# Two products of four column pairs at the head of the up projection, and the first query loads ahead of two stores

## The chip, the cores and the metric

The kernel runs on one core of a Trainium2 chip. The metric is device time in microseconds of one launch. Before the change it is 1542.04 us, the median of three runs (1541.46 to 1542.32). Engines are named as in the profile: PE is TensorE's matmul stream, PEld its weight loads, DVE is VectorE, ACT is ScalarE, POOL is GpSimd, and SP issues nearly all DMAs.

## The reference, cut to what matters

One encoder layer on 1024 prompt frames and 32 sample frames, that is 1056 frames of 1024 features, all in float32:

```
h = rmsnorm(x, g_mix); proj = h @ w_in          # queries, keys, values, conv parts, branch gates
y_attn = stick_breaking(q, k, v) @ w_attn_out;  y_conv = (cb * conv(cc * cx)) @ w_conv_out
x = x + (sigmoid(ga) * y_attn + sigmoid(gc) * y_conv) @ w_o
x = x + square(relu(rmsnorm(x, g_ffn) @ w_up)) @ w_down      # w_up: 1024 x 4096
x = x + sigmoid(rmsnorm(x, g_ple) @ w_ple_gate) * (p @ w_ple)
y = rmsnorm(x, g_final)
```

The change touches the product with w_up and, in its small part, the start of attention.

## The kernel before, in words

**Numbers.** A float32 product is made of three TensorE passes. Each operand is split into a high part (a rounded copy, on ScalarE) and a low part (what is left, a subtraction on VectorE); the passes are high by high, high by low and low by high. So each weight block costs a cast (L107, or L164 for half of one) and a subtraction (L108, L166). In the names `whi` and `wlo`, `sh` and `sl` are these parts.

**Tiles.** Features lie on the 128 partitions, frames in the free dimension. The 1056 frames are two halves of 528, a half is two quarters of 264 (`halves`, `quarters`; t = 0, 1 counts the quarters that belong together).

**The scheme of seven products.** w_up is 1024 x 4096. Two neighbouring blocks of 128 columns are a *set* (or pair); there are 16 sets, u0 to u15. In a set weights and activations are 2 x 2 blocks: A11 and A12 are the even and odd feature blocks of the first column block, A21 and A22 those of the second; B11 and B12 are the even features of the first and the second half of frames, B21 and B22 the odd features. The plain way takes eight block products. The function `seven` (L221) takes seven (Strassen–Winograd) with sums of weights S1 to S4, made on GpSimd by `prepare` (L181, its L203), and sums of activations T1 to T4. A product is 12 matmuls of 128 x 264 (four feature blocks by three passes), and each is done for t = 0 and 1. The order is A11·B11, S1·T1, S2·T2, A12·B21, S3·T3, S4·B22, A22·T4. The product A11·B11 is copied to SBUF as `p1`, and is needed again because S2·T2, S3·T3 and A22·T4 are accumulated in the PSUM bank that holds it (`ps_A11u`). S1·T1 (copied as `s5`) keeps another bank for S4·B22. `u2` is the copy of the first bank after S2·T2. VectorE combines these into the four result blocks C11, C12, C21, C22, in tiles `m1` (first column block) and `m2`; ScalarE takes relu and square, the last block's relu straight from PSUM (`last` is `relu2`, L1467).

**Behind a set.** The down projection is done in the same scheme, so each set also forms its activation sums: `mid_sums` (L1473) does four operations on VectorE, three of them between the two quarters of A22·T4. Blocks and sums are stored to DRAM tiles that `md` names, and read again by the down projection.

**The head of the up projection.** Set 0 is done the plain way (`up_plain`, L1487) with eight block products, 192 matmuls into `ps_up` banks, because the T sums aren't ready when the output projection (w_o, L1385 to L1387, `ps_wo`) ends. Sets 1 to 15 are done with seven. `operands` (L1322) makes the four kinds of B blocks from the residual rows `xr`, one pair of them for each of the eight feature blocks, the last behind the end of the output projection; `square` of the same rows (`sq`) feeds the means for the norm. `mean_squares` (L1443) takes three sums on TensorE, three TENSOR_SCALAR and eight RECIPROCAL on VectorE, starting 14 steps after set 1 has begun.

**What sets the order.** All of it is written out by hand (`manual_schedule`): each engine runs its instructions in the order in which the code emits them. `run` takes a body step by step (a step is a product of one t), and after each step advances each generator in the list `side`: the weight preparation of the next set, whose splits stand at steps given by tables (AT1 for set 1), fetches, T sums, means. A DMA queue of SP is in order as well, so a store that waits for its data holds the loads behind it.

**The start of attention.** The last gate rows of the input projection are stored to DRAM (`gd`, L1129). Then `keys_values` loads the first keys and values, and in the next stage `queries` (L777 to L779) loads the first queries for the scores `z` (L791).

## Time and profile before

| | |
|---|---|
| runs, median | 1542.04 us |
| the profiled execution | 1541.38 us, span 1539.7 us |
| granted TensorE clock, mean | 0.998 |
| busy: PE, DVE, ACT, POOL | 99%, 69%, 49%, 21% of the span |
| DMA | 173 GB/s over the span |

The span runs from the first to the last instruction; the profiled execution's own time is 1.7 us more. The up projection begins 766.4 us into the span. A row of a group of instructions gives line, engine, operation, output and input tile by the program's names with numbers left out (`u0` becomes `u`), partitions x elements, type, and the count. In a row of the timeline the first number is the start in us, the second the duration; in brackets stands the idle time of the engine ahead of it and what ended that. A row of waits gives the idle time, its count and the mean. Line numbers are those of the kernel before, unless it says "of the changed kernel".

### The profile page before, as it was taken

The numbers are of one execution on the slowest core, as the hardware profiler recorded it, in microseconds if no ns is written. First come the engines' busy times: TensorE is split into PE (matmuls) and PEld (weight loads), VectorE is DVE, ScalarE is ACT, GpSimd is POOL, SyncE is SP. The second block draws the span as 40 slices with busy tenths as digits, with TensorE's granted clock in tenths as the row PEclk, the third lists the DMA queues.
The fourth block names the chain that finished last, engine by engine and source line by source line (L and its number), as shares of the span: only waits on it lengthen the run. The fifth ranks groups of instructions, "written<-read, shape, count | busy, mean of one in ns | idle before, by whom it ended". The sixth has DMA issues, their size and how long they took to land.

```text
span 1539.7 us, 29459 instructions
## 1 busy us (share of the span) xinstructions
PE 1518.7 (99%) x11816; PEld 1506.5 (98%) x11816; DVE 1067.1 (69%) x1441; ACT 750.5 (49%) x1371; POOL 317.6 (21%) x340
## 2 busy tenths in 40 slices
PE   8999999999999999999999999999999999999997
PEld 7999999999999999999999999999999999999997
DVE  7568656657578887775577555545577986789756
ACT  6544444434456664432355555555543334434644
POOL 2223322231112221002312222221020220000253
PEclk9999999999999999999999999999999999999999
DMA  6513445413748633445354444344886897683433
GB/s 226 202 48 118 187 153 193 166 44 130 236 125 257 207 123 124 147 167 182 128 191 140 146 147 152 131 143 155 303 281 205 279 332 241 198 275 120 141 127 117
DMA packets 110568, 268.94 MB, mean 175 GB/s; under 512 B 12992, under 2 KB 30144, under 8 KB 110432
## 3 DMA queue, kind: packets, MB, share of 16 engines
q1 hardware_dynamic: 110144, 266.75, 51.3%
q8 instruction: 92, 1.51, 0.4%
q14 instruction: 44, 0.36, 0.1%
q10 hardware_dynamic: 288, 0.32, 0.1%
HBM read 186.31 MB, written 80.72 MB: 173 GB/s over the span
## 4 chain that ended last, share of the span: by engine, by line
PE 63%; DVE 0%; ACT 0%; issue 0%; DVEq 0%
PE ps_dn L1696 7%; PE ps_dn L1698 7%; PE ps_dn L1697 7%; PE ps_A11u L217 4%; PE ps_A11u L216 4%; PE ps_A11u L218 4%; PE ps_pg L116 2%; PE ps_wo L1387 2%; PE ps_wo L1386 2%; PE ps_wo L1385 2%; PE ps_pg L118 2%; PE ps_pg L117 2%; PE ps_S1u L217 2%; PE ps_S1u L218 2%; PE ps_S1u L216 2%; PE ps_oa L116 1%
## 5 line engine op out<-in xcount | busy, mean ns | idle before, releaser
L1698 PE MATMUL ps_dn<-fh,wlo_dn 128*128 128x264 f32 x896 | 255.0, 285 | 0.0
L1696 PE MATMUL ps_dn<-fh,whi_dn 128*128 128x264 f32 x896 | 254.8, 284 | 0.0
L1697 PE MATMUL ps_dn<-fl,whi_dn 128*128 128x264 f32 x896 | 254.5, 284 | 0.0
L1696 PEld LDWEIGHTS ps_dn<-fh,whi_dn 128*128 128x128 f32 x896 | 168.8, 188 | 0.0
L1698 PEld LDWEIGHTS ps_dn<-fh,wlo_dn 128*128 128x128 f32 x896 | 168.6, 188 | 0.0
L1697 PEld LDWEIGHTS ps_dn<-fl,whi_dn 128*128 128x128 f32 x896 | 168.6, 188 | 0.0
L203 POOL TENSOR_TENSOR s_i<-raw_i,raw_i 128x512 f32<-128x512 f32 x32 | 43.6, 1363 | 239.9 <-DVE slS_i L166 209.8
L809 DVE TENSOR_TENSOR_SCAN r<-r 128x128 f32<-128x128 f32 (+3 forms) x64 | 86.4, 1351 | 4.1 <-POOL r L802 4.1
L1583 ACT CAST whi_dn<-raw_dn 128x1024 fp32r<-128x1024 f32 x40 | 42.0, 1051 | 83.5 <-PE ps_dn L1697 83.5
L203 POOL TENSOR_TENSOR s_u<-raw_u,raw_u 128x512 f32<-128x512 f32 x30 | 44.1, 1470 | 182.7 <-DVE slS_u L166 171.0
L1589 DVE TENSOR_TENSOR wlo_dn<-raw_dn,whi_dn 128x1024 fp32r<-128x1024 f32 x40 | 61.3, 1532 | 28.4 <-ACT whi_dn L1583 28.4
L216 PE MATMUL ps_A11i<-T,shS_i 128*128 128x264 f32 x256 | 73.1, 285 | 0.0
L218 PE MATMUL ps_A11i<-T,slS_i 128*128 128x264 f32 x256 | 72.9, 285 | 0.0
L217 PE MATMUL ps_A11i<-T,shS_i 128*128 128x264 f32 x256 | 72.7, 284 | 0.0
L849 DVE TENSOR_TENSOR at<-pa,at 128x512 fp32r<-128x512 f32 (+2 forms) x96 | 52.0, 551 | 26.7 <-ACT at L848 22.2
L1609 DVE TENSOR_TENSOR fl<-mr,fh 128x1056 fp32r<-128x1056 f32 x56 | 70.0, 1249 | 0.3 <-ACT q L1649 0.3
L166 DVE TENSOR_TENSOR slS_i<-s_i,shS_i 128x512 fp32r<-128x512 f32 x48 | 35.1, 737 | 49.7 <-ACT shS_i L164 49.5
L802 POOL TENSOR_SCALAR_AFFINE_SELECT r<-r 128x128 f32<-128x128 f32 x64 | 30.4, 475 | 187.8 <-ACT r L795 176.4
L1780 POOL TENSOR_TENSOR xx<-xx,pgs 128x384 f32<-128x384 f32 (+1 forms) x23 | 24.2, 1057 | 216.8 <-DVE pgs L1779 210.1
L216 PE MATMUL ps_A11u<-T,shS_u 128*128 128x264 f32 x240 | 68.4, 285 | 0.0
L217 PE MATMUL ps_A11u<-T,shS_u 128*128 128x264 f32 x240 | 68.4, 285 | 0.0
L218 PE MATMUL ps_A11u<-T,slS_u 128*128 128x264 f32 x240 | 68.1, 284 | 0.0
(451 smaller groups left out, 5582.9 us busy)
## 6 DMA issues: line engine op xcount, KB each, us to landing
raw_dn<-in_w_down_dram SPq DMA_DIRECT2D x56, 512.0 KB, 4.5
raw_i<-in_w_in_dram SPq DMA_DIRECT2D x36, 512.0 KB, 4.6
mr<-mdT SPq DMA_DIRECT2D x32, 528.0 KB, 5.5
raw_u<-in_w_up_dram SPq DMA_DIRECT2D x32, 512.0 KB, 3.5
mdB<-m SPq DMA_DIRECT2D x48, 264.0 KB, 2.5
mr<-mdB SPq DMA_DIRECT2D x24, 528.0 KB, 6.2
raw_pg<-in_w_ple_gate_dram SPq DMA_DIRECT2D x17, 512.0 KB, 3.6
mdT<-ta SPq DMA_DIRECT2D x32, 264.0 KB, 2.1
```

Of the source, the lines that this page charges most:

```text
L116: nc.tensor.matmul(ps, wh, xh[k][:, cols], start=(k == order[0]), stop=False)
L203: f()
L216: nc.tensor.matmul(p_, wh[:, k, :], o[:, 0, c], start=new and n == 0, stop=False, **on)
L217: nc.tensor.matmul(p_, wh[:, k, :], o[:, 1, c], start=False, stop=False, **on)
L218: nc.tensor.matmul(p_, wl[:, k, :], o[:, 0, c], start=False, stop=z, **on)
L809: nc.vector.tensor_tensor_scan(rev, rev, rev, 1.0, ALU.mult, ALU.bypass)
L849: nc.vector.tensor_tensor(al, pt[:, :nb, :], ah.bitcast(F32), op=ALU.subtract)
L1589: dve(lo, raw, hi.bitcast(F32), op=sub)
L1609: dve(l, mraw.pop(v), opd[v].bitcast(F32), op=sub)
L1696: nc.tensor.matmul(ps, hi[:, j, :], oh, start=j == 0, stop=False)
L1697: nc.tensor.matmul(ps, hi[:, j, :], ol, start=False, stop=False)
L1698: nc.tensor.matmul(ps, lo[:, j, :], oh, start=False, stop=j == NP_ - 1)
```

## The change

**Head of the up projection.** `up_plain` goes; `up_early` takes its place. It does two products of each of the first four sets, which need only B11 and B21: P = A11·B11 and C = A12·B21 on top of it in the same bank, in the order P0, P1, C0, C1, P2, C2, P3, C3. P is copied by ScalarE into a tile that is kept (`pe`, `held_p`). After C the bank holds C11; relu and square are taken, and the block goes to DRAM and is loaded again into `m1` when its set comes. The raw weights are split whole (`early_split`): the first set's in the last block of the output projection, the others' after P0, C1 and P2 of t = 0. The operands B12 are not made any more, and the last feature block's order of B21 and B22 is no longer turned round.

**Sets 0 to 3** then run in `seven`'s new branch with the five other products, 120 matmuls, S1·T1 first; S2·T2 starts a bank of its own. Since the kept P isn't in the bank, it is added or subtracted in SBUF on VectorE: in `s5` and `u2`, and in C21, which VectorE now writes as bank + P (L304 of the changed kernel) before ScalarE takes the relu from SBUF. The weight sums of set 0 are prepared during `up_early`, those of sets 1 to 3 at the steps of a new table AT2. Sets 4 to 15 are as before.

**First queries.** The two stores of the last gate rows are emitted behind the first two calls of `queries`.

```diff
-AT1 = (5, 4, 6, 7, 8, 12)
+AT1 = (5, 4, 6, 8, 10, 12)
+NEARLY = 4
+AT2 = (4, 6, 8, 10, 12, 15)
...
+    def early_split(s_):
+        early_w[s_] = even_odd(load_w(None, 0, KD, f"e{s_}", raw=early_raw.pop(s_)))
+    def early_first(s_, t):
+        p_ = early_ps[s_, t] = products(f"e{s_}_{t}", ((early_w[s_][0], "B11"),), quarters[t])
+        nc.scalar.copy(held_p[s_][:, quarters[t]], p_)
+    def early_second(s_, t):
+        p_ = early_ps.pop((s_, t))
+        products("", ((early_w[s_][1], "B21"),), quarters[t], p_)
+        return p_
...
+        if s_ in held_p:
+            p1 = [held_p[s_][:, quarters[t]] for t in range(2)]
+            for t, a, b in q:
+                z[t] = product("S1", "T1", t)
+                nc.scalar.copy(s5[t], z[t])
+                yield
+            for t, a, b in q:
+                x[t] = product("S2", "T2", t)
+                nc.scalar.copy(u2[t], x[t])
+                dve(s5[t], s5[t], p1[t], op=sub)
+                yield
         for t, a, b in q:
             product("S3", "T3", t, x[t])
+            if s_ in held_p:
+                dve(u2[t], u2[t], p1[t], op=add)
             dve(m2[:, b], x[t], s5[t], op=sub)
...
             product("A22", "T4", t, x[t])
-            last(m2, a, x[t])
+            if s_ in held_p:
+                dve(m2[:, a], x[t], p1[t], op=add)
+                last(m2, a)
+            else:
+                last(m2, a, x[t])
...
         queries(0, 0, 0)
         queries(0, 0, 1)
+        for i, m in enumerate(last_m[1]):
+            nc.sync.dma_start(gd[last_m[0] + i], m)
...
-        by_half = list(zip(halves, ("B21", "B22") if n % 2 else ("B11", "B12")))
-        for c, k in by_half[::-1] if n == KD - 1 else by_half:
+        for c, k in zip(halves, ("B21", "B22") if n % 2 else ("B11",)):
...
-                prepare_plain("u0", 0)
+                early_split("u0")
...
+    def up_early():
+        order = [("P", 0), ("P", 1), ("C", 0), ("C", 1), ("P", 2), ("C", 2), ("P", 3), ("C", 3)]
+        splits = {("P", 0): 1, ("C", 1): 2, ("P", 2): 3}
+        for k, i in order:
...
+            for t in range(2):
+                if k == "P":
+                    early_first(s_, t)
+                else:
+                    p_ = early_second(s_, t)
+                    relu2(c11[i], quarters[t], p_)
+                if t == 0 and (k, i) in splits:
+                    early_split(f"u{splits[k, i]}")
+                yield
+            if k == "C":
+                nc.scalar.square(c11[i], c11[i])
+                nc.sync.dma_start(md("B11", i), c11.pop(i))
...
-        side += [prepare("u1", AT1), all_t(), after(3, call(fetch_up, 2))]
-        run(up_plain())
+        side += [all_t(), after(1, call(fetch_up, 0)), after(3, prepare("u0", AT1)), after(7, call(fetch_up, 1))]
+        run(up_early())
         x1.clear()
         side.append(after(14, mean_squares()))
-        for s_ in range(1, NSET):
+        for s_ in range(NSET):
             if s_ + 1 < NSET:
-                side.append(prepare(f"u{s_ + 1}"))
+                side.append(prepare(f"u{s_ + 1}", AT2) if s_ + 1 < NEARLY else prepare(f"u{s_ + 1}"))
```

Three places in the engines' queues follow; line numbers are those of the kernel that the rows are from. First ScalarE around the end of the output projection. `xr7` is the last residual row, `B22_3` and `B21_3` its operands, `sq7` its square. Before:

```order
L1398 ACTIVATE sq6_9364<-xr6_9015 128x1056
L107 CAST whi_u0_1_9482<-raw_u0_1_9219 128x1024
L1329 ACTIVATE B22_3_9421<-xr7_9121,vecT_98 128x528
L1329 ACTIVATE B21_3_9424<-xr7_9121,vecT_98 128x528
L1398 ACTIVATE sq7_9427<-xr7_9121 128x1056
L1468 ACTIVATE m1_0_9442<-ps_up010_9444 128x264
```

Of the change, where `eu1` is the second pair's weight:

```order
L1442 ACTIVATE sq6_9348<-xr6_9009 128x1056
L1370 ACTIVATE B21_3_9405<-xr7_9115,vecT_98 128x528
L1370 ACTIVATE B22_3_9408<-xr7_9115,vecT_98 128x528
L1442 ACTIVATE sq7_9411<-xr7_9115 128x1056
L220 COPY pe0_9430<-ps_eu0_0_9432 128x264
L109 CAST whi_eu1_9446<-raw_eu1_9312 128x1024
```

The second weight split of the stage stood ahead of the last row's work, and now stands behind it and behind the first copy out of PSUM.

Next VectorE at the end of set 0 of the change: `m2_0` from bank and `pe0` is C21, a quarter at a time; `ta0` and the row that writes `m1_0` are `mid_sums`; `slS2_u1` and `slS3_u1` are low parts for set 1.

```order
L304 TENSOR_TENSOR m2_0_9766<-ps_S2u0_0_9808,pe0_9430 128x264
L168 TENSOR_TENSOR slS2_u1_9923<-s2_u1_9789,shS2_u1_9921 128x512
L1521 TENSOR_TENSOR ta0_9925<-m1_0_9765 128x528
L1523 TENSOR_TENSOR m1_0_9765<-m2_0_9766,m1_0_9765 128x528
L1525 TENSOR_TENSOR ta0_9925<-m1_0_9765 128x528
L304 TENSOR_TENSOR m2_0_9766<-ps_S2u0_1_9824,pe0_9430 128x264
L1528 TENSOR_TENSOR tb0_9926<-m2_0_9766,ta0_9925 128x528
```

Before, the two L304 rows weren't on VectorE; the last relu of a set read the bank on ScalarE. Now the second of them stands behind the three sums.

Then ScalarE at the same place of the change:

```order
L1512 ACTIVATE m2_0_9766<-m2_0_9766 128x264
L166 CAST shS2_u1_9921<-s2_u1_9789 128x512
L1512 ACTIVATE m2_0_9766<-m2_0_9766 128x264
L1515 ACTIVATE m2_0_9766<-m2_0_9766 128x528
L264 COPY s5_u10_9956<-ps_S1u1_0_9958 128x264
L166 CAST shS3_u1_9972<-s3_u1_9790 128x512
L264 COPY s5_u11_9957<-ps_S1u1_1_9980 128x264
L268 COPY u2_u10_9954<-ps_S2u1_0_9995 128x264
```

The relu of C21 now reads SBUF, and behind it in this queue are the square, set 1's copies out of PSUM and its S3 and S4 splits. Before, the rows had the same order with the relu from PSUM.

## The prediction

> **What bounds the kernel now.** I read the totals of the page first, then the stretches, then the waits of TensorE, then the queues around the first up products row by row.

> ```profile
> span 1539.7 us, 29459 instructions
> PE 1518.7 (99%) x11816; PEld 1506.5 (98%) x11816; DVE 1067.1 (69%) x1441; ACT 750.5 (49%) x1371; POOL 317.6 (21%) x340
> ```
> ```profile
> 766.30:790.00 23.70, 23.70 (x197) 1.00 0.47 158
> 850.00:950.00 100.00, 100.00 (x824) 1.00 0.42 145
> ```
> ```profile
> PE z L791 <- DMA q<-qd: 0.5, 1, 0.5
> ```

> TensorE is the bound. Both stretches of the up projection (window, us, busy, matmuls, granted clock, DMA) are full at clock 1.00, so here time is the number of matmuls times their pace. The only wait of TensorE that either edit touches is the last line: 0.5 us for the first queries. So the change can gain matmuls and that wait, and it loses whatever it makes TensorE stand.

> **The matmuls removed.** The rows of the plain first set and the first rows of the next, then two copies that are one steady set apart:

> ```profile
> L216 PE MATMUL ps_up<-B,whi_u x64: 279/284/293, 766.4 to 789.4; 128*128 128x264 f32 x64
> L216 PE MATMUL ps_A11u<-B,whi_u x120: 282/284/552, 789.7 to 1080.8; 128*128 128x264 f32 x120
> ```
> ```profile
> 855.02 0.38 ACT L241 COPY p_u<-ps_A11u 128x264 f32<-128x264 f32 x1 [0.41 <-PE ps_A11u L218]
> 875.46 0.38 ACT L241 COPY p_u<-ps_A11u 128x264 f32<-128x264 f32 x1 [0.40 <-PE ps_A11u L218]
> ```

> The plain set has 3 x 64 = 192 matmuls. A set of seven products has 7 x 2 x 12 = 168, and takes 875.46 - 855.02 = 20.44 us, so 0.1217 us a matmul and 1.46 us a product of 12. Before: 192 + 15 x 168 = 2712. After: 16 x 168 = 2688. The 24 that go are worth 24 x 0.1217 = **-2.9 us**, if TensorE never stands.

> **The queries.** Before, the six query loads stood behind two stores that wait for the last gate rows:

> ```profile
> 392.83 2.28 SPq L1129 DMA_DIRECT2D gd<-m_i  x2
> 397.22 0.59 SPq L779 DMA_DIRECT2D q<-qd  x1
> ```
> ```profile
> 402.17 0.30 PE L791 MATMUL z<-ks,q 128*128 128x128 f32 x1 [0.52 <-DMA q<-qd]
> ```

> The loads can now start once the keys are issued, some us earlier, so the wait ends: **-0.5 us** (bounds 0 and -0.6). The stores move past six loads on SP; their rows are read many us later, so that costs nothing.

> **The two weight splits of the new beginning.** Two pairs' first products take 4 x 1.46 = 5.8 us from 766.4 on; the second pair's split into high and low part must be there after two products, at 769.3. In the queue of ScalarE it now stands behind the work on the last residual row and a copy out of PSUM. The rows of before that price this chain:

> ```profile
> 758.21 0.74 ACT L1329 ACTIVATE B<-xr,vecT 128x528 fp32r<-128x528 f32 x1 [0.82 <-DVE xr L1390]
> 760.61 1.09 ACT L1398 ACTIVATE sq<-xr 128x1056 f32<-128x1056 f32 x1 [1.67 <-DMA td<-xr]
> 766.40 1.06 ACT L107 CAST whi_u<-raw_u 128x1024 fp32r<-128x1024 f32 x1 [4.70 <-PE ps_wo L1386]
> 766.56 0.53 DVE L1390 TENSOR_TENSOR xr<-ps_wo,xr 128x352 f32<-128x352 f32 x1 [3.36 <-PE ps_wo L1387]
> 767.49 1.23 DVE L108 TENSOR_TENSOR wlo_u<-raw_u,whi_u 128x1024 fp32r<-128x1024 f32 x1 [0.41 <-ACT whi_u L107]
> ```

> From the row end at 767.1: B22 0.74 to 767.9, square 1.09 to 768.9, copy 0.38 to 769.2, cast 1.06 to 770.2 (neighbours overlap by 0.1), then VectorE's low part 1.23 to 771.4. The third matmul of the second pair needs it at 769.5: **+2.0 us**. Before, the same split had been put first (766.40) and its use was at 771.2, so it cost nothing. The third pair's split waits for the buffer of the first, which the first's second products release, and stands behind the relu of C1's first half: high part 1.3 us after TensorE has left C1's first product, low part another 1.23, where one product (1.46) covers it: +1.3. At that time GpSimd forms set 0's sums, and a low part that meets one takes 1 us longer (row 815.37 below): **+2.6**, bounds 1.3 and 2.6. The fourth split has four products of cover, so nothing.

> **The ends of the held sets.** A held set has five products, 14.6 us, in place of seven, 20.4 us. What VectorE and ScalarE do in a set:

> ```profile
> 814.70:834.60 19.90, 19.89 (x158) 19.26 (x157) 17.98 (x28) 10.64 (x23) 5.49 (x4) 1.00 0.40 149
> 855.00:875.50 20.50, 20.50 (x170) 20.50 (x170) 10.74 (x17) 11.02 (x22) 5.55 (x5) 1.00 0.43 145
> ```

> (window, us, then busy and count of PE, PEld, DVE, ACT, POOL.) VectorE's 10.7 us lose two adds of 0.43 and one low part of 1.22 and win six 264-wide ops of about 0.42, so about 11.2 of 14.6: enough on average. But the set that takes the eight reciprocals has 18.0, and would need 18.4 in 14.6 us. By that throughput alone 3.8 us are lost. Order makes it worse:

> ```profile
> 813.76 0.40 ACT L1468 ACTIVATE m<-ps_A11u 128x264 f32<-128x264 f32 x1
> 814.19 0.65 ACT L1471 ACTIVATE m<-m 128x528 f32<-128x528 f32 x1
> 814.99 0.62 ACT L164 CAST shS_u<-s_u 128x512 fp32r<-128x512 f32 x1
> 815.78 0.39 ACT L245 COPY s_u<-ps_S1u 128x264 f32<-128x264 f32 x1
> ```
> ```profile
> 814.64 0.70 DVE L1477 TENSOR_TENSOR ta<-m 128x528 f32<-128x528 f32 x1
> 815.37 1.67 DVE L1479 TENSOR_TENSOR m<-m,m 128x528 f32<-128x528 f32 x1
> 817.08 0.71 DVE L1481 TENSOR_TENSOR ta<-m 128x528 f32<-128x528 f32 x1
> 818.95 0.68 DVE L166 TENSOR_TENSOR slS_u<-s_u,shS_u 128x512 fp32r<-128x512 f32 x1
> 823.25 0.97 DVE L1455 RECIPROCAL rs<-rs 128x132 f32<-128x132 f32 x1
> ```
> ```profile
> 811.51 1.29 POOL L203 TENSOR_TENSOR s_u<-raw_u,raw_u 128x512 f32<-128x512 f32 x1 [15.09 <-DVE slS_u L166]
> 814.86 1.62 POOL L203 TENSOR_TENSOR s_u<-raw_u,raw_u 128x512 f32<-128x512 f32 x1 [0.69 <-DVE slS_u L166]
> ```

> Before, ScalarE took the last relu of a set straight from PSUM (813.76), whatever VectorE did. Now VectorE must first add the kept product (L304 of the changed kernel), and for the second quarter that add stands behind three sums of halves in VectorE's queue. ScalarE's relu waits for it, and behind the relu wait the next set's copies out of PSUM and its S3 split. Also, 815.37 is 1.67 instead of 0.70 because it met the GpSimd row at 814.86.

> I lay this out from 0, the start of the next set's first product. VectorE's add of the first quarter ends at -0.8; relu 0.38 and the S2 cast 0.61 on ScalarE to 0.1; low part 0.69 to 0.9; that ends GpSimd's wait (as at 811.51), so its first two sums of the set after next run now. VectorE: 0.70 to 1.5, 1.67 to 3.2, the third sum to 3.9 free or 4.8 met by GpSimd's second; the add 0.43 to 5.2; ScalarE: relu 0.4, square 0.65, copy 0.39, cast 0.62, copy 0.39, then the copy of S2's product at 7.7. TensorE wants to add S3 onto that bank after four products, at 5.84, and so stands 2.0 us (1.1 free of the second collision).

> So: end of set 0: 2.0. End of set 1: the same, 0.8 later through the three rows of the means, 2.8; the S3 low part stands behind one reciprocal, 0.6; then five reciprocals (0.88 apart), its own 0.6 and seven ops of 3.1 together lie before the last split's end, 8.0 us where TensorE has 5.9 us of products, 2.1. End of set 2: 2.0 and about 1.3 of reciprocals not yet done, 3.3. End of set 3: 2.0. Sum **+12.8 us**; bounds: 3.8 (throughput alone, everything else hidden), 12.8. I take the upper end less 1.5, since the rows of before, laid end to end in the same way, give 1.4 us of standing around 809 and 819 that the trace doesn't have: **+11.3**.

> The 264-wide ops on two SBUF tiles are in no row: from below 0.3 (half of a 528-wide one), from above 1.5 (met by GpSimd). I use 0.42, the same width out of PSUM. [...]

> Removed work (four B12 operands, set 0's plain half) frees ScalarE and VectorE where neither was late: nothing. The four C11 blocks go out to DRAM and come back; 264 KB land in 2 to 3 us, and they have 13: nothing.

> **The sum.** The profiled execution took 1541.4 us around its span of 1539.7, 0.6 under the median of the runs, 1542.0. 1541.4 - 2.9 - 0.5 + 2.0 + 2.6 + 11.3 = 1553.9; against the spread of the runs I say **1553.5**.

> **The rivals.** (1) VectorE runs far enough ahead that the set ends stay hidden, and only the two splits show: 1541.4 - 3.4 + 4.6 = 1542.6, no change. For it: on average VectorE has 3 us to spare a set. Against it: the queue's order, and the eight reciprocals. Chance 0.07. (2) All is hidden: 1541.4 - 3.4 = 1538.0, faster. It holds if the second split is ready by 769.5, and is decided by where ScalarE's cast stands: before the square and the copy it would end at 769.0, behind them it can't. Chance 0.05. (3) The set ends cost only throughput: 1541.4 - 3.4 + 4.6 + 3.8 = 1546.4, slower still; part of my case's lower side. (4) The pauses, up to 3.3 us, cool the array.

> ```profile
> 8.00:10.00 2.00, 2.00 (x11) 2.00 (x11) 1.77 (x6) 2.00 (x6) 0.00 (x0) 1.00 1.06 360
> ```

> After the 6 us of standing at the start, 11 matmuls ran in 2 us where 16.4 fit: 0.7 us lost, though some of it to operands. Three such: 1555.6. Gaps of up to 1.0 us later cost nothing like it. [...] Chance 0.06.

> **How the numbers follow.** My case with (3) in it has 0.82. The range goes from (3), 1546.0, to (4) and the unlaid collisions, 1557.0. About 0.2%, 3 us, is what a measurement of this kernel tells from no change. Faster: (2), 0.05. Within: (1), 0.07. Slower: 0.82 + 0.06 = 0.88.

> **What would show it.** Right: 192 matmuls again in the beginning, but 4 to 5 us longer, with waits for the second and third weight split; at each held set's end an idle of 2 us or more before S3's first matmul, ended by ScalarE's copy of S2's product, and one before A22 in the set with the reciprocals; sets from 5 on at 20.4 us. The z matmul starts without a wait. Wrong: held sets of 14.6 to 15 us, or ScalarE's last relu of a set within 1 us of the product.

## The result and the profile after

The changed kernel takes 1559.07 us (median of five runs, 1558.96 to 1560.72), the kernel before 1542.32 us beside it (1541.46 to 1543.01). The ratio is 1.0112, with a 95% interval of 1.0097 to 1.0126: 1.1% slower, 16.8 us. The forecast was slower, 1553.5 us with a range of 1546 to 1557, so the direction held and the size did not.

The profiled execution took 1559.43 us around a span of 1557.7. First the totals of the changed kernel's page, then the stretch from the first up product to the first down product, of before and of after (window, us, then busy and count of PE, PEld, DVE, ACT, POOL, then granted clock, DMA share, GB/s).

```profile
span 1557.7 us, 29489 instructions
PE 1525.4 (98%) x11792; PEld 1509.8 (97%) x11792; DVE 1084.8 (70%) x1463; ACT 750.6 (48%) x1378; POOL 325.1 (21%) x344
```

```profile
766.36:1098.70 332.34, 332.33 (x2720) 331.32 (x2719) 191.83 (x281) 184.91 (x350) 77.66 (x56) 1.00 0.46 159
```

```profile
767.00:1116.49 349.49, 337.57 (x2696) 333.94 (x2695) 214.08 (x307) 187.07 (x360) 91.62 (x64) 0.99 0.45 160
```

The 24 matmuls are gone, and the up projection is 17.15 us longer, nearly all of the 18.0 us by which the span grew. The rest is scatter of the two executions and the down projection, which is 0.5 us longer. So 17.15 + 2.92 = 20.07 us are to be found. The waits of TensorE in that stretch, and below them the stretches of 3.41 us around three places where the granted clock is 0.50:

```profile
PE ps_S2u L239 <- ACT u_u L268: 4.4, 3, 1.8
PE ps_eu L241 <- DVE wlo_eu L110: 2.6, 2, 1.9
PE ps_S2u L241 <- DVE slA_u L168: 1.9, 1, 1.9
PE ps_A11u L239 <- ACT shS_u L166: 1.3, 1, 1.3
PE ps_eu L239 <- ACT whi_eu L109: 0.8, 1, 0.8
PE ps_S2u L241 <- DVE slS_u L168: 0.3, 1, 0.3
PE ps_eu L239 <- ACT pe L220: 0.3, 1, 0.3
PE ps_A11u L241 <- DVE slS_u L168: 0.2, 1, 0.2
```

```profile
769.47:772.88 3.41, 1.82 (x13) 1.39 (x12) 3.19 (x4) 2.32 (x6) 0.00 (x0) 1.00 0.99 291
772.88:776.29 3.41, 3.41 (x18) 3.41 (x17) 3.38 (x5) 1.51 (x3) 0.00 (x0) 0.50 0.99 377
817.26:820.67 3.41, 1.65 (x14) 1.44 (x13) 2.62 (x4) 3.31 (x8) 1.11 (x1) 1.00 0.75 256
820.67:824.08 3.41, 3.41 (x15) 2.91 (x14) 3.41 (x6) 0.00 (x0) 1.57 (x2) 0.50 0.20 72
844.57:847.98 3.41, 1.55 (x12) 1.34 (x12) 3.41 (x8) 1.64 (x3) 0.00 (x0) 1.00 0.56 154
847.98:851.39 3.41, 3.41 (x17) 3.41 (x17) 2.99 (x6) 1.68 (x5) 0.00 (x0) 0.50 0.64 233
```

All but two are waits that the forecast had named: not named were the 0.3 us for the copy of P, and the wait at the end of set 3, which the forecast had put before an S3 and which stands before S2 of set 4, mostly for ScalarE's cast (1.3 us in the list). By the steps from one matmul's start to the next, less the 0.122 us of the steady pace, the pauses come to 13.7 us: 4.4 in the head and 9.3 at the ends of the held sets. The three stretches of half clock were not in the sum: in each, 15 to 18 matmuls ran where 28 fit, at 0.220 us a matmul instead of 0.122, which loses about 1.5 us each and 4.6 together. The last 1.8 us are mostly the first matmul behind each pause, which takes 0.23 us instead of 0.12, some fourteen times. 13.7 + 4.6 + 1.8 - 2.9 = 17.2.

The chain at the end of a held set, at the end of set 0, VectorE, then ScalarE, then TensorE (start, duration):

```profile
811.68 0.69 DVE L168 TENSOR_TENSOR slS_u<-s_u,shS_u 128x512 fp32r<-128x512 f32 x1 [1.00 <-ACT shS_u L166]
812.29 0.70 DVE L1521 TENSOR_TENSOR ta<-m 128x528 f32<-128x528 f32 x1
813.03 1.68 DVE L1523 TENSOR_TENSOR m<-m,m 128x528 f32<-128x528 f32 x1
814.75 1.68 DVE L1525 TENSOR_TENSOR ta<-m 128x528 f32<-128x528 f32 x1
816.35 0.42 DVE L304 TENSOR_TENSOR m<-ps_S2u,pe 128x264 f32<-128x264 f32 x1
...
821.72 1.50 DVE L292 TENSOR_TENSOR u_u<-u_u,pe 128x264 f32<-128x264 f32 x1
```

```profile
816.80 0.42 ACT L1512 ACTIVATE m<-m 128x264 f32<-128x264 f32 x1 [5.15 <-DVE m L304]
817.26 0.64 ACT L1515 ACTIVATE m<-m 128x528 f32<-128x528 f32 x1
817.81 0.36 ACT L264 COPY s_u<-ps_S1u 128x264 f32<-128x264 f32 x1
818.07 0.62 ACT L166 CAST shS_u<-s_u 128x512 fp32r<-128x512 f32 x1
818.59 0.38 ACT L264 COPY s_u<-ps_S1u 128x264 f32<-128x264 f32 x1
818.86 0.39 ACT L268 COPY u_u<-ps_S2u 128x264 f32<-128x264 f32 x1
```

```profile
819.30 0.39 PE L239 MATMUL ps_S2u<-T,shS_u 128*128 128x264 f32 x1 [1.76 <-ACT u_u L268]
```

The low part of S2 lets GpSimd begin, two of the three sums take 1.68 instead of 0.71 us, the add of the second quarter stands behind them, ScalarE waits 5.15 us for it, and set 1's copies stand behind that relu. At this end of set 0 it is the layout of the prediction, row by row.

### The profile page after: what moved, and what is told of

It is laid out like the page before. It is cut to its first block, busy times and chain, and to the rows that moved or that the text cites. A ratio compares the mean times of both kernels' runs of the same rounds, so it can differ in the third digit from the quotient of the medians.

```text
span 1557.7 us, 29489 instructions
## 1 busy us (share of the span) xinstructions
PE 1525.4 (98%) x11792; PEld 1509.8 (97%) x11792; DVE 1084.8 (70%) x1463; ACT 750.6 (48%) x1378; POOL 325.1 (21%) x344
## 5 line engine op out<-in xcount | busy, mean ns | idle before, releaser
L1512 ACT ACTIVATE m<-m 128x528 f32<-128x528 f32 (+1 forms) x52 | 31.8, 611 | 92.0 <-DVE m L293 30.0
L239 PE MATMUL ps_A11i<-T,shS_i 128*128 128x264 f32 x256 | 73.0, 285 | 0.0
L241 PE MATMUL ps_A11i<-T,slS_i 128*128 128x264 f32 x256 | 72.9, 285 | 0.0
L1431 PE MATMUL ps_wo<-mh,wlo_wo 128*128 128x352 f32 x192 | 62.1, 324 | 0.0
L1430 PE MATMUL ps_wo<-ml,whi_wo 128*128 128x352 f32 x192 | 62.1, 323 | 0.0
```

Source lines behind the costliest of these rows:

```text
L239: nc.tensor.matmul(p_, wh[:, k, :], o[:, 0, c], start=new and n == 0, stop=False, **on)
L241: nc.tensor.matmul(p_, wl[:, k, :], o[:, 0, c], start=False, stop=z, **on)
L1430: nc.tensor.matmul(ps, hi[:, k, :], ml[k][:, c], start=False, stop=False, skip_group_check=True)
L1431: nc.tensor.matmul(ps, lo[:, k, :], mh[k][:, c], start=False, stop=k == KD - 1, skip_group_check=True)
```

## The experiments

**The order at the set ends, the means, and the clock.** Four runs of the changed kernel with an edit follow. The first adds work, to fill the pauses, and takes nothing away. The second and the third take one suspected cause each, and the fourth goes on from the third.

```diff
+    def keep_busy(n):                     # n matmuls of ones on ones
...
+        if s_ in ("u1", "u2", "u3"):
+            keep_busy(4)                  # ahead of S3
+        if s_ == "u1":
+            keep_busy(4)                  # ahead of A22
+                    if t == 0 and i in (1, 2):
+                        keep_busy(4)      # ahead of P1 and P2
```

> The changed kernel with 24 matmuls of ones on ones added in six places where TensorE waits anyway (4 each: ahead of the second and third pair's first product, ahead of S3 in sets 1, 2 and 3, ahead of A22 in set 1; 4 took 1.09 us at the end of the trace before). Nothing else changes, the results are the same. Theory (the clock): the changed kernel lost about 4.9 us in three spells of some 3.4 us at a pitch of 0.22 us instead of 0.122, each behind pauses of 1.9 to 2.0 us; they come because TensorE was idle for more than half of a stretch of 3.41 us. The added matmuls leave every pause under 1.3 us, so all three spells go: about 1554 us, though work is added. Rival (the spells come from the waits' end or from traffic, not from idle time): they stay, and the time is 1559 us or up to 2 us more for matmuls that don't fit into their pause.

Measured 1560.35 us, ratio to before 1.0122 (1.0106 to 1.0138): not faster. The expected time failed, for two reasons that the trace shows. The wait before A22 is in set 2, not in set 1, so that filler stood in the wrong set; the unfilled pause of 2.0 us again had its stretch of half clock (850.47 to 853.88). And a pause of 3.2 us came in at 793, where C3 waited for ScalarE's copy of P3 (`PE ps_eu L239 <- ACT pe L220: 3.0, 1, 3.0`) behind two casts of T that were late, one of them for its load:

```profile
788.29 0.63 ACT L161 CAST T<-rt 128x528 fp32r<-128x528 f32 x1 [1.93 <-DMA rt<-td]
788.83 0.39 ACT L1521 ACTIVATE ce<-ps_eu 128x264 f32<-128x264 f32 x1
791.19 0.63 ACT L161 CAST T<-rt 128x528 fp32r<-128x528 f32 x1 [1.97 <-issue]
...
792.79 0.36 ACT L220 COPY pe<-ps_eu 128x264 f32<-128x264 f32 x1
```

In the changed kernel's own trace C3 lost 0.4 us to that copy. Two stretches of half clock followed the pause of 3.2 us. Behind the filled pauses (P1, and S3 of sets 1 to 3) there was none, where the changed kernel had two; the mean granted clock is 0.995 in both profiled runs. So the run speaks for idle time as the cause, but its time decides nothing; the cause was measured by itself below.

```diff
-        side.append(after(14, mean_squares()))
+        side.append(after(50, mean_squares()))
```

> The changed kernel with the means (three sums, three TENSOR_SCALAR, eight reciprocals) started 50 steps behind the head instead of 14, in the sets of seven products. Theory: the reciprocals in VectorE's queue make the wait before A22 in set 1 (2.0 us), the 0.5 us before S3's low part, and the slow spell behind them (1.6 us): 2.5 to 4.1 us less, 1555 to 1556.6. The pauses before S3 stay. Rival: VectorE has time to spare and the reciprocals only fill it; the pause is the order of the sums: within 0.5 us of 1559.

Measured 1557.3 us, ratio 1.0100 (1.0082 to 1.0118), 0.7 us short of the theory's range. The waits say why:

```profile
PE ps_S2u L239 <- ACT u_u L268: 7.5, 3, 2.9
PE ps_eu L239 <- ACT pe L220: 2.5, 2, 1.7
```

The waits for the low parts of A22 and S3 are gone, as expected, and only one stretch of half clock is left in the up projection (mean granted clock 0.997 over the span, 0.995 in the changed kernel). But the three waits for ScalarE's copy at the set ends grew from 4.4 to 7.5 us: in the changed kernel, it seems, the pauses and the slow stretches before them had let VectorE and ScalarE catch up. Removing one pause uncovered the next in the same queue. 2.2 us more went to the late copy of P in the head.

```diff
-            if t == 0:
+            if t == (1 if s_ in held_p else 0):
                 done("near")              # the three sums of halves
```

> The changed kernel with C21's second add in the held sets ahead of the three sums of halves on VectorE, instead of behind them. Theory: ScalarE's relu and copies come 4 us earlier, so no wait for ScalarE's copy of S2 is left; but next in line is VectorE's low part of S3, now behind the sums, which comes 1.5 to 2.5 us late in sets 1 to 3, so most of the pauses (6.8 us in four places) stay under another name: 2 to 4 us less, 1555 to 1557. Rival (the order of that add is the whole cause of the pauses at the ends): they go, 1559.1 - 6.8 = 1552 or less.

Measured 1554.7 us, ratio 1.0085 (1.0069 to 1.0101): 4.4 us less than the changed kernel, a little more than the 2 to 4 expected.

```profile
PE ps_S2u L241 <- DVE slS_u L168: 2.8, 3, 1.8
PE ps_S2u L241 <- DVE slA_u L168: 1.9, 1, 1.9
```

No wait for ScalarE's copy of S2 is left; the pauses are there under the name of VectorE's low part of S3, which now stands behind the sums. That is the theory; the rival, by which the add's place alone makes the pauses, would have given 1552 or less.

```diff
-AT2 = (4, 6, 8, 10, 12, 15)
+AT2 = (4, 5, 7, 8, 10, 13)               # on top of the add first
```

> The add first, as in the run before, and the splits of the next held set's weight sums one to two steps earlier (4, 5, 7, 8, 10, 13 in place of 4, 6, 8, 10, 12, 15), so that S3's low part also stands ahead of the three sums. Theory (order, not throughput): the pauses before S3 of sets 1 and 2 go; those that the reciprocals make stay or move by a product: 5 to 8 us less, 1551 to 1554. Rival (VectorE's throughput in sets of 14.6 us, or GpSimd's collisions, set the pauses): they move to other waits of the same size, and the time stays above 1556.

Measured 1550.3 us, ratio 1.0057 (1.0041 to 1.0072): 8.8 us less than the changed kernel, slightly more than the 5 to 8 expected. About 3 us of that are the clock, by an estimate from the 1.5 us a stretch above, since the up projection of the profiled run has one stretch of half clock (783.14 to 786.55) in place of three. No wait before S3 of sets 1 and 2 is left, nor the one before A22 beside the reciprocals. Set 3 and set 4 still wait 2.9 us (the rows below are those of the ends of the held sets, then a stretch in the columns used above):

```profile
PE ps_S2u L239 <- ACT u_u L268: 1.6, 1, 1.6
PE ps_A11u L241 <- DVE wlo_u L110: 0.7, 1, 0.7
PE ps_A11u L241 <- DVE slS_u L168: 0.6, 1, 0.6
```
```profile
825.00:850.00 25.00, 23.25 (x187) 22.63 (x185) 23.30 (x34) 12.57 (x27) 10.49 (x7) 1.00 0.40 136
```

So most of what the ends lost was order in two queues. For what is left, VectorE's amount of work isn't excluded: it was busy for 23.3 of the 25.0 us that hold the reciprocals, and the chain to the copy that S3 of set 3 waits for begins behind the last of them. In the changed kernel, too, VectorE had 18.3 us of work in the set with the reciprocals, where the five products need 14.6; the pauses had stretched that set to 20.5. No run here takes order and amount of work fully apart, since the runs below that have no wait left at the set ends also move the means out of the held sets.

**The clock by itself.** Two kernels put pauses of known length into sets 4 to 14 of the kernel before; the second fills them.

```diff
+    def pause(n, src):
+        scr = wpool[0].tile([P, 192], F32, tag="scr", name="scr", bufs=1)
+        for i in range(n):
+            pool(scr, src if i == 0 else scr, src, op=add)
+        ps = tps.tile([P, 512], F32, tag="tp", name="ps_pause")
+        for _ in range(0):                # second kernel: 3 * n
+            nc.tensor.matmul(ps[:, :P], ones, ones, start=True, stop=True)
+        nc.tensor.matmul(ps[:, :P], ones, scr[:, :P], start=True, stop=True)
+    PAUSE = {f"u{i}": 2 + i % 3 for i in range(4, 15)}
...
             nc.scalar.copy(u2[t], x[t])
+            if t == 1 and s_ in PAUSE:
+                pause(PAUSE[s_], u2[1][:, :192])
```

> The kernel before, with a pause put into each of sets 4 to 14: behind the product S2 of the second quarter TensorE waits for a small matmul whose operand GpSimd makes by two, three or four adds in a row (128 x 192, in turn over the sets), which it starts when ScalarE has copied that product. Results are the same. The pauses should last about 2 to 3.5 us and add some 29 us in all (11 x 0.6 for the copy and the restart, 34 adds of about 0.65). Theory (the clock falls when TensorE was idle for more than about half of a fixed stretch of 3.41 us): besides the pauses about 7 of the 11 are followed by a spell of 3.4 us at half pace, 1.5 us each, some 10 us more: 1541 + 29 + 10 = 1580. The spells begin and end at multiples of 3.41 us from each other, whichever the pause. Rival (the slow spells of the changed kernel come from its traffic or its operands): no spells here, 1570 us.

> The same pauses in the same places, each filled with 6, 9 or 12 matmuls of ones on ones (about 0.2 us each) ahead of the waiting one, so that TensorE is busy for most of the pause and idle for about 1 us. Theory of the clock: the pauses last as long as in the run before, no spell follows, about 10 us less than the run before, though it does 102 matmuls more. Rival: the same time as the run before, or a little more.

Measured 1582.45 us (ratio 1.0268, 1.0254 to 1.0282) and 1574.76 us (1.0218, 1.0204 to 1.0232): the filled kernel does 102 matmuls more and is 7.7 us faster. The pauses are as long in the one as in the other, but TensorE's waits in them come to 27.4 us in the first and 4.7 in the second. In the up projection the first kernel has four stretches of half clock in its profile, not the seven expected, the second none; four times about 1.5 us is close to the 5.8 us by which the two profiled executions differ (1580.70 and 1574.87). The runs of the first scatter over 3.9 us, those of the second over 0.8. So in these two kernels the idle time brings the half clock, and not the traffic or the operands of the changed kernel. Which pauses brought them was not expected. The unfilled kernel, in stretches of 3.41 us counted from those at half clock:

```profile
860.79:864.20 3.41, 1.02 (x8) 0.81 (x8) 0.69 (x1) 1.64 (x3) 1.68 (x3) 1.00 0.23 89
864.20:867.61 3.41, 3.41 (x17) 3.41 (x17) 0.27 (x1) 0.00 (x0) 0.00 (x0) 0.50 0.16 65
884.68:888.09 3.41, 1.87 (x16) 1.66 (x14) 0.69 (x1) 2.23 (x4) 0.91 (x2) 1.00 0.14 23
888.09:891.51 3.42, 1.85 (x15) 1.86 (x16) 0.00 (x0) 0.00 (x0) 1.35 (x3) 1.00 0.37 133
891.51:894.92 3.41, 3.41 (x30) 3.41 (x29) 2.29 (x4) 1.31 (x3) 0.00 (x0) 1.00 0.19 29
```

The pauses lasted 1.94, 2.60 and 3.27 us by turns. All four of about 2.60 were followed by 3.41 us at half clock; none of the four of 3.27 and none of the three of 1.94 was. The first row holds a whole pause (2.55 us); the third and fourth share one of 3.27 us, 1.70 and 1.56 idle. In these rows the half clock goes with how much of one stretch is idle, not with how long the pause is. That each length always fell in the same place is an accident of this kernel: three sets with their pauses last 71.7 us, which is 21 stretches.

**The queries alone.** The move of the two stores, in the kernel before.

> The kernel before with the first query loads ahead of the two stores of the last gate rows, and nothing else. Theory: the wait of the first scores on the query load (0.5 us) is gone from the trace, and the stretch from the last A22 product of the input projection to the first scores is 0.5 to 0.8 us shorter; in the time of one run this is hardly to be told. Rival: the loads wait for the keys' loads or for the write of the queries instead, and the stretch stays 8.0 us.

A single run: 1540.68 us beside 1541.24, within the scatter. No wait of the first scores is in the list of waits any more, and the 60 matmuls from the last product of the input projection to the first scores take 7.31 us in place of 7.99; the changed kernel has 7.31 too. This part did what it says, 0.7 us.

**A version in another order.** The same products and the same matmuls as in the change, with the queues put in order:

```diff
+        early_split("u1")                 # ahead of the last row's operands
         wo_after(KD - 1)
-        splits = {("P", 0): 1, ("C", 1): 2, ("P", 2): 3}
+        splits = {("C", 0, 1): 2, ("P", 2, 1): 3}
-        side += [all_t(), after(1, call(fetch_up, 0)), after(3, prepare("u0", AT1)), ...
+        side += [after(5, all_t()), after(3, call(fetch_up, 0)), after(5, prepare("u0", AT1)), ...
...                                       # also: the add first; AT2 = (4, 5, 7, 8, 10, 13);
...                                       # the means after 50; set 4 at (5, 6, 7, 9, 11, 15)
```

> The changed kernel, reordered: C21's second add ahead of the sums and the earlier splits as in the fourth run; the means 50 steps later; the second pair's split ahead of the last residual row's operands, the third's behind C0, the fourth's behind P2; the T sums five steps later and set 0's weight sums later with their load; set 4's splits a step or two earlier. Theory (all that the change lost was order in the queues): the up stage is 2.9 us shorter than before but for some 1.5 us of small waits, the queries give 0.5, no slow spell: 1541.3 - 2.9 - 0.5 + 1.5 = 1539.4. Rival (the loads of the T sums, which were late in the first four runs by 0.4 to 3 us, are now what the beginning waits for, with a slow spell behind it): 1541 to 1545.

Measured 1543.6 us beside 1541.2, ratio 1.0017 (1.0008 to 1.0026): of the change's loss of 16.8 us 2.4 are left. It is still slower than before, and the time lies in the rival's range, not at the theory's 1539.4. Nothing is left at the set ends; in the head TensorE still waits 3.1 us:

```profile
PE ps_eu L241 <- DVE wlo_eu L110: 2.0, 2, 1.4
PE ps_eu L239 <- ACT pe L220: 1.1, 1, 1.1
```

But it isn't the loads that the rival named, and no slow stretch follows. By the rows of the two queues, VectorE stood idle for 5.5 us because the sums of the last T operands had been moved back with the casts, then the third split's low part took 2.30 us instead of 1.23, as the one did that met GpSimd in the changed kernel (2.29), and ScalarE's cast and the copies behind it waited for those sums. The next two kernels start the sums in the second step and keep only the casts late:

```diff
+            for _ in range(1):
+                yield
             raw_t[KD // 2 - 1] = sums(KD // 2 - 1, e, o)
-            yield
+            for _ in range(5):            # 4 in the second
+                yield
-        splits = {("C", 0, 1): 2, ("P", 2, 1): 3}
+        splits = {("C", 0, 1): 2, ("P", 2, 0): 3}     # ("P", 2, 1) in the second
```

> The reordered kernel of the eighth run with three edits: the sums behind the last T operands start in the second step, in the 5.5 us that VectorE idled there, and the casts of T five steps after them; the fourth pair's split one product earlier again; the load of set 0's second weights stays at step 3. Theory: of the three waits that the eighth run had left in the beginning (0.8, 1.2 and 1.5 us) only the first stays; the up stage is 2 to 2.9 us shorter than before, no spell of half clock in the profiled run: 1538 to 1540. Rival (the loads of T and of weights on the one queue are the bound of the beginning, and order only moves the wait): 1541 to 1544, as in the eighth run.

> The same, with the casts of T four steps behind the sums and the fourth pair's split behind P2's second half. Theory: within 1 us of the run before. Rival: the copy of P2 comes late behind the split or the casts, 1 to 2 us more than the run before.

Measured 1540.7 and 1540.6 us, ratios 0.9998 (0.9989 to 1.0007) and 0.9996 (0.9987 to 1.0005). The two are alike, as the second expectation had it, and lie between the theory and the rival of the first. The waits went as the theory said: the first has one of 0.5 us in the head and one of 0.2 us in set 0, the second one of 1.7 us in the head. But the up projection of the first is only 1.1 us shorter than before (331.28), where 2 to 2.9 were expected.

The last two change the order of the head's products, so that each weight buffer comes free earlier:

```diff
-        order = [("P", 0), ("P", 1), ("C", 0), ("C", 1), ...
+        order = [("P", 0), ("C", 0), ("P", 1), ("C", 1), ...
+        splits = {("P", 0, 0): 1, ("C", 0, 1): 2, ("C", 1, 1): 3}
...                                       # second kernel: the last row's square one step later,
...                                       # and with it the sums of the last T operands
```

> The reordered kernel with the head's products in the order P0, C0, P1, C1, P2, C2, P3, C3, so that each pair's weight buffers come free two products earlier, and each split (behind P0, C0 and C1) has four products, 5.8 us, before its use in place of two; the second pair's split is back behind the last residual row. Theory: the covers were the last thing missing. No wait for a low part in the head, the up stage 2 to 3.5 us shorter than the 332.3 us before, the time 1537.5 to 1539.5. Rival: C now follows its P at once, so that ScalarE's copy of P has one product (1.5 us) and not three to be done; TensorE waits for it behind the square (1.1 us) and behind casts, 1 to 2 us in all: 1540 to 1542.

> The same, with the square of the last residual row one step later, behind the copy of P0's first half. If ScalarE's copy is what is waited for in the run before, this is about 1 us faster; if not, the two are the same within 0.5 us.

Measured 1540.0 us (ratio 0.9992, 0.9983 to 1.0001) and 1540.1 us (0.9995, 0.9986 to 1.0004). The head has no wait in either, as the theory had it, and the rival's wait for the copy of P isn't there; yet the time is the rival's lower end and not the 1537.5 to 1539.5 of the theory. The two are the same within 0.5 us, so ScalarE's copy wasn't what the first waited for in the head. The first has a wait of 1.9 us in set 0 instead, behind casts of T that waited for their loads. The second, whose sums of T come a step later as well, has none in the whole up projection:

```profile
766.30:1096.95 330.65, 330.65 (x2696) 329.75 (x2695) 210.88 (x307) 187.52 (x360) 91.02 (x64) 1.00 0.49 169
```

That is 1.7 us less than the 332.34 before, where 24 matmuls are worth 2.9. The difference is pace: 330.65 us over 2696 matmuls are 0.1226 us each here, and 332.34 over 2720 were 0.1222 before, which over the 2696 is 1.2 us. Why is open. Both medians gain 1.2 to 1.3 us, half of what these 1.7 and the queries' 0.7 would make, and the intervals don't exclude no change. So the change's idea is worth some 0.1% here by the medians, 0.2% at the most by the intervals, and only when nothing waits.

## Why the prediction was wrong, point by point

**The matmuls removed, -2.9 us.** Right in number (11816 to 11792), and reached nowhere in full: the stretch without a wait still gained only 1.7, since its matmuls ran at a slightly slower pace.

**The queries, -0.5 us.** Right; 0.7 by the trace.

**The two splits, +2.0 and +2.6 us.** The second pair's pauses are 1.0 and 0.9 us, 1.9 as priced. The third's is 2.0: VectorE's low part met GpSimd and took 2.29 us, as supposed. "The fourth split has four products of cover, so nothing" held for the split, but the copy of P3 behind it was late by 0.4 us, for a T load that no step of mine had looked at; in other runs this was up to 3.2. Together 4.4 for 4.6.

**The ends of the held sets, +11.3 us.** The mechanism was right, at set 3's end with another row (the cast for S2 of set 4, not the copy before an S3), and the size was 2.0 too high: 1.9 for 2.0 at the end of set 0, 3.8 for 5.5 at set 1, 1.7 for 3.3 at set 2, 1.9 for 2.0 at set 3. My layout started each end as late as the one before, and the pauses and slow stretches in between probably gave VectorE and ScalarE time back, as the second experiment suggests from the other side. The 264-wide operations on two SBUF tiles took 0.42 free, as taken, and 1.50 when they met GpSimd, my upper bound. The "unlaid collisions" in the upper end of my range are a term that no run shows as such; what the changed kernel shows in its place are single rows, 1.50 us for L292 at 821.72 and 0.93 for L269 at 840.28, each beside a GpSimd sum.

**The clock, taken as nothing.** This is the step that failed. I set it aside as rival (4), with 0.06, by "gaps of up to 1.0 us later cost nothing like it". The runs show that pauses of the length I had listed can do it: in the changed kernel, behind three stretches of 3.41 us with 1.9 to 2.0 us of idle time, one of them made of two pauses, the granted clock fell to 0.50, which cost 4.6 us, and the restarts cost some 1.5 more that I hadn't counted either. Predicted pauses, less the matmuls, gave +13.0 in the up projection; with the pauses as measured (13.7) it would have been +10.8, and the missing 6.4 are clock and restarts. That the forecast missed by no more than 5.6 us is partly luck: pauses put 2.2 us too high made up for a third of the 6.4. Had I put rival (4) into the sum, 0.7 us for each of the seven pauses that I had listed at 2 us or more, the forecast would have been 4.9 us later, 1558.4, close to the time but by seven cases at 0.7 where there were three at 1.5. The price was too low since the row that I took from the start of the kernel covered 2 us of half pace and not 3.41, and counted 11 matmuls where 9 began. Nor was any of it owed to operands: the row prints a clock of 1.00, but the matmuls in it stand 0.22 us apart, as in the stretches at 0.50.

**The rivals.** (1) and (2), that all or nearly all is hidden, fell with the direction; (2) was come near to (1540.0 for 1538.0) only when two queues and the head were put in another order. (3), the ends at their throughput alone, fell for this kernel, whose ends lost 9.3 us and not 3.8. Yet the fourth experiment, with the order put right and the reciprocals in place, still waits 2.9 us there, so a price of that kind isn't refuted; with the means moved out as well nothing is left.

## What to carry to other kernels

Removing 24 matmuls from a bound engine gained less (1.7 us) than one late relu cost (1.9): where a kept value is added on another engine, ask first what stands ahead of that add and behind the instruction that waits for it. Price a pause of a busy TensorE by its length, and then read the granted clock behind it: here three pieces of idle time of 1.9 to 2.0 us cost a further 1.5 us each, while pauses of 3.27 us that lay across two stretches cost none. After removing a wait look at the next in the same queue: two edits here mostly renamed one, until the order was right in both queues at once.

## What the runs showed of the hardware

```profile
783.12:786.53 3.41, 1.67 (x13) 1.67 (x14) 3.41 (x4) 1.85 (x5) 0.60 (x1) 1.00 0.47 102
786.53:789.95 3.42, 3.42 (x31) 3.42 (x30) 2.33 (x4) 3.42 (x8) 0.00 (x0) 1.00 1.05 372
```

It is the third split's pause of 2.0 us: 1.7 of it fell into the first of these stretches, and the second is at full clock.

Two of VectorE's sums of halves took 1.68 us each in the changed kernel while GpSimd worked (813.03 and 814.75, beside its sums of 1.64 us at 812.51 and 814.23), and 0.71 where it didn't:

```profile
872.03 0.71 DVE L1523 TENSOR_TENSOR m<-m,m 128x528 f32<-128x528 f32 x1
872.77 0.71 DVE L1525 TENSOR_TENSOR ta<-m 128x528 f32<-128x528 f32 x1
```
